# Three weight tiles side by side where a layer begins behind a norm

## The chip, the cores and the metric

One Trainium2 chip, one of its cores. The metric is the device time of one execution in microseconds (us); the median of three executions of the kernel before is 1987.98 us (1987.56 to 1994.38).

## The reference, cut to what matters

Two transformer-like blocks on 512 positions of 1024 features, all in float32. The first block is a pooling layer and a latent-attention layer; the second has an attention and an RWKV mixer that start from one normed input, and a convolutional feed-forward layer (ffn) behind a second norm. The change touches the two places of the second block where a norm is followed by large projections:

```python
h = rms_norm(x, norm1_w[l]) * (1.0 + sc1) + sh1
proj = h @ w_in[l]                      # mixers: 3 low-rank tiles of it are computed first
...
h = rms_norm(x, norm2_w[l]) * (1.0 + sc2) + sh2
x = x + gt2 * conv_ffn(h, w_up[l], conv_w[l], conv_b[l], w_down[l])   # starts with h @ w_up
```

## The kernel before, in words

Activations are held transposed: a tile has 128 features on the partitions and the 512 positions as columns, so 1024 features are eight tiles. To reach float32 accuracy every operand is split into a high part (rounded to TensorE's fp32r) and a low part (the rest), and each product is three matmuls: high weight x high activation (L176), high x low (L177), low x high (L178). One output tile over eight input tiles is 24 matmuls of 512 columns.

Weights come as chunks of 128x1024 (512 KB). `wload` (L137 and on) has SP transfer a chunk into one of three buffers "wraw", lets ScalarE copy it to "whi" (L160) and VectorE subtract to "wlo" (L161), both at high priority; whi and wlo have two buffers each. So up to three chunks are under way or waiting and two are split. The instructions' order on every engine and queue is set by a planner: it plays the program through and takes, of what is ready on an engine, what stands first in the program; what is written under `high_priority()` goes ahead of the rest. A tile's buffer is given when its first instruction is taken, and on the chip each engine and queue then runs its list in order. Pages of 128x512 come from pools that are opened and closed by stage: `pg1` (46 pages) up to the end of `Block2In.finish`, `pg4` (61 pages) from `attn_out` on. Between them lie the mixer's pools.

A norm works in halves of 256 columns: sums of squares (`Sums.add`, L318 and L320), column sums on TensorE (`norm_sum`, L262), root and reciprocal (`norm_end`), and the result spread over all partitions by a matmul with a diagonal (`spread`, L290 and L293) into a PSUM bank "ch". `modulate` then makes each of the eight tiles' high and low part: VectorE L738, ScalarE L739, VectorE L743. In the first norm three tiles of each half have the low part done by GpSimd (L742) behind an extra ScalarE pass (L741).

`gemm_head` is what follows. It loads the chunks of two output tiles with the subtraction on GpSimd instead of VectorE, and multiplies them half by half, one output tile after the other, into the two PSUM banks "mm". Further tiles follow over the full width, in the banks "sc": one (w_rw 26) in the mixers' head, two (w_up 2 and 3) in the ffn's, of which the first has its split in four pages "xwh" and "xwl", with the subtractions on GpSimd (L228). The results are taken from PSUM by `feat` (L816, L817) in the mixers and by `conv` (L1482 to L1484) in the ffn.

Ahead of the first head, `mla_layer` does the last output projections (`project`, chunks of w_mout), the last two of them in halves (`gemm_tail`). Ahead of the second, `attn_out` multiplies eight tiles by w_o, the last two in halves; its x comes by eight transfers "xf" into pages.

Of the kernel before, what the change touches and what calls it, by code (L numbers as in the profile page):

```python
# [9 lines left out]
AF = mybir.ActivationFunctionType  # L10
ALU = mybir.AluOpType
# [38 lines left out]
def f(ap):  # L50
    return ap.bitcast(F32)


class Kern:
# [155 lines left out]
                self.gemm_w(w, acts, ps[:, 0:S // 2], ts)  # L210
                evac(n, ps[:, 0:S // 2], ts)

    def gemm_head(self, wname, chunks, kts, acts, more=(), page=None):

        ws = []
        for c in chunks:
            ws.append(self.wchunks(wname, c, kts, self.nc.gpsimd))

        extra = None
        if page is not None:  # L220
            nc = self.nc
            raw = self.wp.tile([P, D], F32, name="wraw", tag="wraw")
            nc.sync.dma_start(raw, self.a[wname][more[0]][:, :D])
            extra = []
            for h in range(2):
                hi, lo, r = page(F32R, "xwh"), page(F32R, "xwl"), raw[:, h * S:h * S + S]
                nc.scalar.activation(hi, r, AF.Copy)
                nc.gpsimd.tensor_tensor(lo, r, f(hi), ALU.subtract)  # L228
                extra.append((hi, lo, 4))
        out = [self.mm() for _ in chunks]  # L230
        for ts in HALVES:
            for w, ps in zip(ws, out):
                self.gemm_w(w, acts, ps[:, ts], ts)
        for c in more:
            ps = self.bank("sc")
            self.gemm_w(extra or self.wchunks(wname, c, kts), acts, ps)
            extra = None
            out.append(ps)
        return out

    def gemm_multi(self, wname, chunk, kt, nt, acts, evac, n0):
# [234 lines left out]
def mla_layer(K, xs, mi, z_scr, done, after, filler=lambda h: None):  # L476
# [193 lines left out]
    def project(q, c, ys):  # L670

        K.gemm_multi("w_mout", 4 * q + c, 4, 2, ys[4 * q:4 * q + 4], evac_last if q == 3 else evac_x, 2 * c)
# [10 lines left out]
    for g in range(8):  # L683
        rope_split(*qrs[g])
        if g % 2 and g < 7:
            qrs += rope_q(g // 2 + 1)
        heads(g, o, ys)
        if g < 7:
            o = gemms(g + 1)
        if g == 7:  # L690
            flush()
            while vals:
                vals.pop(0)(None)
        for q, c in PROJ[g]:
            project(q, c, ys)
    for c in range(2):
        project(3, c, ys)
    ws = []
# [31 lines left out]
    nc.vector.scalar_tensor_tensor(K.A2, K.ada[:, 32:40], 1.0, K.v("norm2_w", 0, 8), ALU.add, ALU.mult)  # L730


def modulate(K, x, A, inv, sh, hl, ts=FULL, pool=False):

    nc = K.nc
    t = K.page(name="mod")[:, ts]
    hi, lo = hl[0][:, ts], hl[1][:, ts]
    nc.vector.scalar_tensor_tensor(t, x[:, ts], A, inv, ALU.mult, ALU.mult)  # L738
    ins = nc.scalar.activation(hi, t, AF.Identity, bias=sh)  # L739
    if pool:  # L740
        nc.scalar.activation(t, t, AF.Identity, bias=sh)  # L741
        return ins, nc.gpsimd.tensor_tensor(lo, t, f(hi), ALU.subtract)  # L742
    return ins, nc.vector.scalar_tensor_tensor(lo, t, sh, f(hi), ALU.add, ALU.subtract)  # L743


class Block2In:
# [10 lines left out]
    def finish(self):  # L757

        K, xs = self.K, self.xs
        nc = K.nc  # L760
        fa = K.const.tile([P, 8], F32, name="fa1")
        nc.vector.tensor_tensor(fa, K.A1, K.v("final_norm", 0, 8), ALU.mult)
        hs = [(K.apage("hh"), K.apage("hl")) for i in range(DT)]
        r1s = K.const.tile([P, 4], F32, name="r1s")
        hh = []
        for h, ts in enumerate(HALVES):

            nps = K.norm_sum([self.s1.last(), self.s2.last()], ts)
            ss = K.sm.tile([P, 2], F32, name="ss", tag="ss")
            with K.tc.high_priority():  # L770
                ins = nc.vector.tensor_scalar(ss, nps[:, 0:2], EPS, EPS * EPS * D, ALU.mult, ALU.add)
                for a in hh[2:3]:
                    K.behind(ins, a[1])
                nc.vector.tensor_tensor(ss, ss, nps[:, 2:4], ALU.add)
            r12 = K.norm_end(ss, D, 2, 0.0, [a[0] for a in hh[1:2]])
            inv12 = K.spread(r12, 2)
            nc.vector.tensor_copy(r1s[:, 2 * h:2 * h + 2], nps[:, 0:2])
            for i in range(DT):
                hh.append(modulate(K, xs[i], fa[:, i:i + 1], inv12, K.ada[:, i:i + 1], hs[i], ts, i in ((2, 4, 6), (1, 3, 5))[h]))
        r1s = K.norm_end(r1s, D)  # L780
        inv1 = K.spread(r1s)
        for i in range(DT):
            xf = K.page(name="xf")
            nc.vector.scalar_tensor_tensor(xf, xs[i], K.v("final_norm", i), inv1, ALU.mult, ALU.mult)
            nc.sync.dma_start(K.x_scr[i], xf)
        return hs


def rwkv(K, hs, filler=lambda: None):
# [19 lines left out]
    def feat(n, ps=None):  # L809

        if ps is None:
            ps = K.mm()
            K.gemm_n("w_rw", n, [8], hs, ps)
        z = K.page(name="zm")
        with K.tc.high_priority():
            nc.scalar.activation(z, ps, AF.Copy, scale=omu[:, n:n + 1])  # L816
            nc.vector.scalar_tensor_tensor(z[:, 1:], ps[:, :S - 1], K.v("mu", n), z[:, 1:], ALU.mult, ALU.add)  # L817
        return z

    pss = K.gemm_head("w_rw", (24, 25), [8], hs, (26,))  # L820
    zs_ = [feat(24 + i, ps) for i, ps in enumerate(pss)]

    lw = zs_[0]
    nc.scalar.activation(lw[0:64], lw[0:64], AF.Tanh)
# [617 lines left out]
def attn_out(K, mg, xscr):  # L1442

    nc = K.nc
    xs, xf = [], []
    acc = Sums(K)
    for n in range(DT):
        t = K.page(name="xf")
        nc.sync.dma_start(t, xscr[n])
        xf.append(t)  # L1450
        xs.append(K.page(name="x"))

    def evac(n, ps, ts=FULL):
        nc.vector.scalar_tensor_tensor(xs[n][:, ts], ps, K.ada[:, 16 + n:17 + n], xf[n][:, ts], ALU.mult, ALU.add)
        acc.add(n, xs[n], ts=ts)

    for n in range(DT - 2):
        ps = K.mm()
        K.gemm_n("w_o", n, [8], mg, ps)
        evac(n, ps)  # L1460
    K.gemm_tail([(n, K.wchunks("w_o", n, [8])) for n in (DT - 2, DT - 1)], mg, evac, acc.last())
    return xs, acc


def ffn(K, xs, acc):

    nc = K.nc
    hs = [(K.apage("hh"), K.apage("hl")) for i in range(DT)]
    for ts in HALVES:
        inv = K.rstd(acc.last(), D, ts)  # L1470
        for i in range(DT):
            modulate(K, xs[i], K.A2[:, i:i + 1], inv, K.ada[:, 24 + i:25 + i], hs[i], ts)

    def conv(n, ps=None):

        ci = (n % 2) * 22 + n // 2
        if ps is None:
            ps = K.mm()
            K.gemm_n("w_up", n, [8], hs, ps)
        t = K.page(name="cv")  # L1480
        w = [K.v("conv_w", j * 44 + ci) for j in range(3)]
        nc.scalar.activation(t, ps, AF.Identity, scale=w[2], bias=K.v("conv_b", ci))  # L1482
        nc.vector.scalar_tensor_tensor(t[:, 1:], ps[:, :S - 1], w[1], t[:, 1:], ALU.mult, ALU.add)
        nc.vector.scalar_tensor_tensor(t[:, 2:], ps[:, :S - 2], w[0], t[:, 2:], ALU.mult, ALU.add)  # L1484
        return t

    pss = K.gemm_head("w_up", (0, 1), [8], hs, (2, 3), K.page)
    for half in range(2):
        act = []
        for i in range(11):  # L1490
            n = 2 * (half * 11 + i)
            gt = conv(n, pss[n] if n < 4 else None)
            vl = conv(n + 1, pss[n + 1] if n < 4 else None)
            sg = K.page(name="sg")
            nc.scalar.activation(sg, gt, AF.Silu)
            a = K.page(name="fa")
            nc.vector.tensor_tensor(a, sg, vl, ALU.mult)
            act.append(K.split(a, "fa"))
        if half == 0:
            out = []  # L1500
            for n in range(DT):
                ps = K.mm()
                K.gemm_n("w_down", 2 * n, [6, 5], act, ps)
                x = K.page(name="x")
                nc.vector.scalar_tensor_tensor(x, ps, K.ada[:, 40 + n:41 + n], xs[n], ALU.mult, ALU.add)
                out.append(x)
            xs = out
    acc = Sums(K)
    xw = [K.page(name="xw") for n in range(DT)]

    def evac(n, ps, ts=FULL):
        x = xs[n][:, ts]
        nc.vector.scalar_tensor_tensor(x, ps, K.ada[:, 40 + n:41 + n], x, ALU.mult, ALU.add)  # L1513
        acc.add(n, xs[n], ts=ts)
        nc.gpsimd.tensor_scalar(xw[n][:, ts], x, K.v("norm_f_w", n), None, ALU.mult)

    for n in range(DT - 1):
        ps = K.mm()
        K.gemm_n("w_down", (DT + n) * 2, [6, 5], act, ps)
        evac(n, ps)  # L1520
    K.gemm_tail([(DT - 1, K.wchunks("w_down", (2 * DT - 1) * 2, [6, 5]))], act, evac, acc.last())
    return xw, acc
# [296 lines left out]
```

## Time and profile before

| | |
|---|---|
| median of three executions | 1987.98 us |
| the profiled execution | 1989.22 us |
| its span | 1987.4 us |
| TensorE matmul busy | 1915.4 us (96%) |
| VectorE busy | 1272.3 us (64%) |
| ScalarE busy | 890.4 us (45%) |
| GpSimd busy | 111.0 us (6%) |

The times that are argued with come from the profiled execution: positions are microseconds from the start of its span. In the profile PE is TensorE, PEld its weight loads, DVE is VectorE, ACT is ScalarE, POOL is GpSimd, and SP (SPq) is the queue that issues transfers. A timeline line has the start, the duration, the engine, the line of the code, the operation, output and inputs, sizes and count, and in brackets the engine's idle time before it and what ended it. Matmuls are pipelined, so their duration is longer than the distance of their starts.

### The profile page before, as it was taken

The page shows a single profiled execution, that of the slowest core. Times are in us where ns is not written, and L with a number is a line of the kernel's source. Part 1 is how long each engine was busy: PE and PEld are TensorE (multiplying, and loading weights), DVE is VectorE, ACT ScalarE, POOL GpSimd, SP SyncE. Part 2 cuts the span into 40 slices and gives each one's busy share as a digit, 9 for nine tenths or more (in the row PEclk, how much of TensorE's full clock was granted, in tenths as well). Part 3 has the DMA queues.
Part 4 walks back from the last instruction along what each step waited for, and adds up shares of the span by engine and source line. Part 5 has one row for each costly group of instructions (what it writes and reads, how often), then busy time and mean ns, then how long its engine had stood idle before and what let it go on. Part 6 is the DMA issues. An engine that isn't in the chain of part 4 may idle for free. (4 is left out here: it accounts for less than half of the span.)

```text
span 1987.4 us, 28348 instructions
## 1 busy us (share of the span) xinstructions
PE 1915.4 (96%) x10759; PEld 1553.2 (78%) x10771; DVE 1272.3 (64%) x2284; ACT 890.4 (45%) x1602; POOL 111.0 (6%) x221
## 2 busy tenths in 40 slices
PE   8999999999999998999999999989999999999998
PEld 6888887887888887777777866767777888888886
DVE  6746777768866668676567477466456576535654
ACT  5322333336655546543445555555642344423432
POOL 0000000000000002110030030020000010000002
PEclk9999999999999999999999999999999999999999
DMA  4332365675422223643443433334355423233322
GB/s 166 98 103 96 95 200 182 208 238 176 130 85 75 77 68 128 200 133 97 152 137 113 145 120 123 133 112 144 130 191 182 152 75 97 89 101 106 96 84 86
DMA packets 97496, 254.55 MB, mean 128 GB/s; under 512 B 11216, under 2 KB 15824, under 8 KB 97360
## 3 DMA queue, kind: packets, MB, share of 16 engines
q1 hardware_dynamic: 96848, 251.51, 39.6%
q8 instruction: 85, 1.39, 0.3%
q0 software_dynamic: 224, 0.79, 0.1%
q10 hardware_dynamic: 288, 0.45, 0.1%
q14 instruction: 51, 0.42, 0.1%
HBM read 212.59 MB, written 37.75 MB: 126 GB/s over the span
## 5 line engine op out<-in xcount | busy, mean ns | idle before, releaser
L160 ACT ACTIVATE whi<-wraw 128x1024 fp32r<-128x1024 f32 (+4 forms) x302 | 299.1, 991 | 592.2 <-PE mm L177 373.8
L161 DVE TENSOR_TENSOR wlo<-wraw,whi 128x1024 fp32r<-128x1024 f32 (+4 forms) x298 | 338.3, 1136 | 196.3 <-ACT whi L160 192.6
L177 PE MATMUL mm<-hl,whi 128*128 128x512 f32 (+1 forms) x992 | 393.5, 397 | 4.0 <-DVE hl L743 3.7
L176 PE MATMUL mm<-hh,whi 128*128 128x512 f32 (+1 forms) x992 | 389.8, 394 | 0.0
L178 PE MATMUL mm<-hh,wlo 128*128 128x512 f32 (+1 forms) x992 | 388.0, 392 | 0.0
L177 PEld LDWEIGHTS mm<-hl,whi 128*128 128x128 f32 x992 | 189.2, 191 | 42.8 <-DVE hl L743 4.3
L176 PEld LDWEIGHTS mm<-hh,whi 128*128 128x128 f32 x992 | 189.1, 191 | 38.1 <-issue 2.0
L178 PEld LDWEIGHTS mm<-hh,wlo 128*128 128x128 f32 x992 | 189.5, 191 | 35.7 <-issue 2.2
L176 PE MATMUL mm<-xgh,whi 128*128 128x512 f32 x432 | 170.2, 394 | 7.5 <-ACT xgh L342 7.1
L177 PE MATMUL mm<-xgl,whi 128*128 128x512 f32 x432 | 171.0, 397 | 0.7 <-DVE xgl L343 0.7
L178 PE MATMUL mm<-xgh,wlo 128*128 128x512 f32 x432 | 169.4, 392 | 0.0
L176 PEld LDWEIGHTS mm<-xgh,whi 128*128 128x128 f32 x432 | 81.9, 190 | 25.6 <-ACT xgh L342 7.1
L176 PE MATMUL mm<-yh,whi 128*128 128x512 f32 (+1 forms) x256 | 98.3, 384 | 0.0
L177 PE MATMUL mm<-yl,whi 128*128 128x512 f32 (+1 forms) x256 | 98.1, 383 | 0.0
L178 PE MATMUL mm<-yh,wlo 128*128 128x512 f32 (+1 forms) x256 | 98.0, 383 | 0.0
L177 PEld LDWEIGHTS mm<-xgl,whi 128*128 128x128 f32 x432 | 81.9, 190 | 19.2 <-DVE xgl L343 1.6
L178 PEld LDWEIGHTS mm<-xgh,wlo 128*128 128x128 f32 x432 | 81.7, 189 | 18.0 <-issue 1.0
L720 DVE SCALAR_TENSOR_TENSOR adaw<-adaw,cb 128x1024 f32<-128x1024 f32 x48 | 58.7, 1223 | 33.6 <-DMA adaw<-in_w_ada 32.4
L177 PE MATMUL mm<-fal,whi 128*128 128x512 f32 (+1 forms) x176 | 67.3, 383 | 0.0
L178 PE MATMUL mm<-fah,wlo 128*128 128x512 f32 (+1 forms) x176 | 67.3, 383 | 0.0
L176 PE MATMUL mm<-fah,whi 128*128 128x512 f32 (+1 forms) x176 | 67.3, 382 | 0.0
L658 ACT ACTIVATE p<-sc,nm 128x128 f32<-128x128 f32 (+1 forms) x64 | 33.7, 527 | 58.2 <-DVE nm L655 46.1
(422 smaller groups left out, 3541.2 us busy)
## 6 DMA issues: line engine op xcount, KB each, us to landing
adaw<-in_w_ada SPq DMA_DIRECT2D x48, 512.0 KB, 4.1
wraw<-in_w_up SPq DMA_DIRECT2D x44, 512.0 KB, 3.6
wraw<-in_w_at SPq DMA_DIRECT2D x36, 512.0 KB, 3.7
wraw<-in_w_pin SPq DMA_DIRECT2D x32, 512.0 KB, 3.6
wraw<-in_w_rw SPq DMA_DIRECT2D x27, 512.0 KB, 4.0
wraw<-in_w_min SPq DMA_DIRECT2D x22, 512.0 KB, 4.4
a_scr<-aqkv SPq DMA_DIRECT2D x36, 256.0 KB, 2.2
aq<-a_scr SPq DMA_DIRECT2D x36, 256.0 KB, 3.7
```

The source lines that it names most:

```text
L160: nc.scalar.activation(hi, raw, AF.Copy)
L161: eng.tensor_tensor(lo, raw, f(hi), ALU.subtract)
L176: nc.tensor.matmul(out, wh, ah, start=first, stop=False)
L177: nc.tensor.matmul(out, wh, al, start=False, stop=False)
L178: nc.tensor.matmul(out, wl, ah, start=False, stop=last)
L658: nc.scalar.activation(p[:, :nk], sc[:, :nk], AF.Exp, bias=nm, scale=scale, accum_out=sm)
L720: nc.vector.scalar_tensor_tensor(w, w, 1.0, K.cb, ALU.mult, ALU.mult, accum_out=K.ada[:, i:i + 1])
```

## The change

`head_weights` is new. It transfers three chunks and splits each into two high and two low pages, on ScalarE and VectorE, at high priority; it is called well ahead of its use: in `mla_layer` before the last output projections (w_rw 24, 25, 26), and in `attn_out` after the second of the eight w_o tiles (w_up 0, 1, 2). `gemm_head` takes these, and computes three output tiles side by side in halves: for every input tile all three output tiles' matmuls, into the two "mm" banks and one "sc" bank. In the mixers it is called inside `Block2In.finish`, directly behind the modulation. The ffn's fourth tile (w_up 3) goes the ordinary way. `modulate` loses its GpSimd form.

```diff
-    def gemm_head(self, wname, chunks, kts, acts, more=(), page=None):
+    def head_weights(self, wname, chunks, page):
+
+        nc = self.nc
         ws = []
         for c in chunks:
-            ws.append(self.wchunks(wname, c, kts, self.nc.gpsimd))
...
             raw = self.wp.tile([P, D], F32, name="wraw", tag="wraw")
-            nc.sync.dma_start(raw, self.a[wname][more[0]][:, :D])
-            extra = []
+            nc.sync.dma_start(raw, self.a[wname][c][:, :D])
+            w = []
             for h in range(2):
                 hi, lo, r = page(F32R, "xwh"), page(F32R, "xwl"), raw[:, h * S:h * S + S]
-                nc.scalar.activation(hi, r, AF.Copy)
-                nc.gpsimd.tensor_tensor(lo, r, f(hi), ALU.subtract)
-                extra.append((hi, lo, 4))
-        out = [self.mm() for _ in chunks]
+                with self.tc.high_priority():
+                    nc.scalar.activation(hi, r, AF.Copy)
+                    nc.vector.tensor_tensor(lo, r, f(hi), ALU.subtract)
+                w.append((hi, lo, 4))
+            ws.append(w)
+        return ws
+
+    def gemm_head(self, ws, acts):
+
+        out = [self.mm(), self.mm(), self.bank("sc")][:len(ws)]
         for ts in HALVES:
-            for w, ps in zip(ws, out):
-                self.gemm_w(w, acts, ps[:, ts], ts)
-        for c in more:
-            ps = self.bank("sc")
-            self.gemm_w(extra or self.wchunks(wname, c, kts), acts, ps)
-            extra = None
-            out.append(ps)
+            for ci in range(2):
+                for j in range(4):
+                    sl = slice(j * P, (j + 1) * P)
+                    k = ci * 4 + j
+                    for w, ps in zip(ws, out):
+                        hi, lo, _ = w[ci]
+                        self.mm3(ps[:, ts], hi[:, sl], lo[:, sl], acts[k][0][:, ts], acts[k][1][:, ts], k == 0, k == 7)
         return out
...
         for q, c in PROJ[g]:
             project(q, c, ys)
+    K.head = K.head_weights("w_rw", (24, 25, 26), K.page)
     for c in range(2):
         project(3, c, ys)
...
-    if pool:
-        nc.scalar.activation(t, t, AF.Identity, bias=sh)
-        return ins, nc.gpsimd.tensor_tensor(lo, t, f(hi), ALU.subtract)
...
+        K.heads = K.gemm_head(K.head, hs)
         r1s = K.norm_end(r1s, D)
...
-    pss = K.gemm_head("w_rw", (24, 25), [8], hs, (26,))
-    zs_ = [feat(24 + i, ps) for i, ps in enumerate(pss)]
+    zs_ = [feat(24 + i, ps) for i, ps in enumerate(K.heads)]
...
         evac(n, ps)
+        if n == 1:
+            K.head = K.head_weights("w_up", (0, 1, 2), K.page)
...
-    pss = K.gemm_head("w_up", (0, 1), [8], hs, (2, 3), K.page)
+    pss = K.gemm_head(K.head, hs)
...
-            gt = conv(n, pss[n] if n < 4 else None)
-            vl = conv(n + 1, pss[n + 1] if n < 4 else None)
+            gt = conv(n, pss[n] if n < 3 else None)
+            vl = conv(n + 1, pss[n + 1] if n < 2 else None)
```

## Rows read from the trace of the kernel before

**Rows 1.** The page, busy time of each engine, its share and its instructions.
```profile
PE 1915.4 (96%) x10759; PEld 1553.2 (78%) x10771; DVE 1272.3 (64%) x2284; ACT 890.4 (45%) x1602; POOL 111.0 (6%) x221
```
**Rows 2.** Windows: length, busy time by engine (instructions), granted clock, DMA share, GB/s.
```profile
755.40:761.70 6.30, 1.58 (x7) 1.10 (x7) 6.30 (x16) 3.08 (x6) 2.46 (x1) 0.82 0.42 120
761.70:784.60 22.90, 21.86 (x130) 19.49 (x130) 20.43 (x43) 14.68 (x30) 4.64 (x6) 0.90 0.27 93
1606.50:1631.47 24.97, 21.29 (x128) 19.59 (x127) 20.74 (x40) 12.27 (x22) 6.02 (x4) 0.86 0.27 78
1610.00:1615.00 5.00, 4.44 (x20) 4.37 (x21) 4.01 (x11) 2.35 (x6) 0.23 (x1) 0.50 0.36 111
```
**Rows 3.** Timeline of TensorE, attn_out and the ffn's head.
```profile
1571.82 0.39 PE L176 MATMUL mm<-mh,whi 128*128 128x512 f32 x1
...
1610.56 0.58 PE L177 MATMUL mm<-hl,whi 128*128 128x256 f32 x1 [1.87 <-DVE hl L743]
...
1616.92 0.60 PE L293 MATMUL ch<-dg,ones 128*128 128x256 f32 x2
...
1621.06 0.28 PE L177 MATMUL mm<-hl,whi 128*128 128x256 f32 x1
1621.18 0.28 PE L178 MATMUL mm<-hh,wlo 128*128 128x256 f32 x1
...
1631.47 0.39 PE L176 MATMUL sc<-hh,whi 128*128 128x512 f32 x1
1631.70 0.39 PE L177 MATMUL sc<-hl,whi 128*128 128x512 f32 x1
```
**Rows 4.** Timeline of VectorE, the ffn's head.
```profile
1605.15 2.47 DVE L320 TENSOR_TENSOR sq<-sq 128x256 f32<-128x256 f32 x1
...
1608.33 2.18 DVE L743 SCALAR_TENSOR_TENSOR hl<-mod,ada,hh 128x256 fp32r<-128x256 f32 x1
...
1620.72 0.47 DVE L738 SCALAR_TENSOR_TENSOR mod<-x,A,ch 128x256 f32<-128x256 f32 x1
1621.11 0.47 DVE L743 SCALAR_TENSOR_TENSOR hl<-mod,ada,hh 128x256 fp32r<-128x256 f32 x1
```
**Rows 5.** Timeline of GpSimd, the ffn's head.
```profile
1607.76 2.46 POOL L161 TENSOR_TENSOR wlo<-wraw,whi 128x1024 fp32r<-128x1024 f32 x1 [0.42 <-ACT whi L160]
```
**Rows 6.** Timeline of VectorE, the mixers' head.
```profile
757.88 2.16 DVE L320 TENSOR_TENSOR sq<-sq 128x256 f32<-128x256 f32 x1
```
**Rows 7.** Half a chunk: tile xwh's copies (ns, min/median/max), VectorE's timeline for a subtraction.
```profile
L227 ACT ACTIVATE xwh<-wraw x2: 617/618/618, 1623.2 to 1624.1; 128x512 fp32r<-128x512 f32 x2
...
1634.86 0.69 DVE L171 TENSOR_TENSOR fal<-fa,fah 128x512 fp32r<-128x512 f32 x1 [0.70 <-ACT fah L170]
```
**Rows 8.** Timeline of ScalarE, a result taken from PSUM in the ffn.
```profile
1643.29 0.76 ACT L1482 ACTIVATE cv<-mm,vec 128x512 f32<-128x512 f32 x1
```
**Rows 9.** Timeline of VectorE, a result taken from PSUM in the ffn.
```profile
1644.56 0.74 DVE L1483 SCALAR_TENSOR_TENSOR cv<-mm,vec,cv 128x511 f32<-128x511 f32 x1
```
**Rows 10.** The page, DMA issues: count, KB each, median us from issue to landing.
```profile
wraw<-in_w_up SPq DMA_DIRECT2D x44, 512.0 KB, 3.6
```
**Rows 11.** Windows, as in rows 2, the last attention heads.
```profile
705.00:710.00 5.00, 4.78 (x42) 4.33 (x41) 3.91 (x14) 3.14 (x10) 0.00 (x0) 1.00 0.17 52
```
**Rows 12.** Timeline, first instructions on tiles of the mixer's new pools.
```profile
790.13 0.33 SPq L90 DMA_DIRECT2D gmask<-in_gmask  x1
790.15 0.31 ACT L96 ACTIVATE bonr<-cst 128x128 fp32r<-128x128 f32 x1 [3.95 <-DMA wraw<-in_w_g]
```
**Rows 13.** Timeline of SP, the end of the mixers and attn_out.
```profile
1548.72 14.78 SPq L148 DMA_DIRECT2D wraw<-in_w_o  x5
...
1565.82 3.65 SPq L1449 DMA_DIRECT2D xf<-x_scr  x8
1569.57 10.39 SPq L148 DMA_DIRECT2D wraw<-in_w_o  x3
```
**Rows 14.** Tile wraw, the one transfer issued from 1569.3 to 1574 us (us, min/median/max).
```profile
DMA to landing us min/median/max: 6.4/6.4/6.4
```

More of the change, by code (lines that the diff above doesn't have):

```diff
@@ L211, in gemm_tail @@
                 evac(n, ps[:, 0:S // 2], ts)
-    def gemm_head(self, wname, chunks, kts, acts, more=(), page=None):
+    def head_weights(self, wname, chunks, page):
+        nc = self.nc
         ws = []
         for c in chunks:
-            ws.append(self.wchunks(wname, c, kts, self.nc.gpsimd))
-        extra = None
-        if page is not None:
-            nc = self.nc
             raw = self.wp.tile([P, D], F32, name="wraw", tag="wraw")
-            nc.sync.dma_start(raw, self.a[wname][more[0]][:, :D])
-            extra = []
+            nc.sync.dma_start(raw, self.a[wname][c][:, :D])
+            w = []
             for h in range(2):
                 hi, lo, r = page(F32R, "xwh"), page(F32R, "xwl"), raw[:, h * S:h * S + S]
-                nc.scalar.activation(hi, r, AF.Copy)
-                nc.gpsimd.tensor_tensor(lo, r, f(hi), ALU.subtract)
-                extra.append((hi, lo, 4))
-        out = [self.mm() for _ in chunks]
-        for ts in HALVES:
-            for w, ps in zip(ws, out):
-                self.gemm_w(w, acts, ps[:, ts], ts)
-        for c in more:
-            ps = self.bank("sc")
-            self.gemm_w(extra or self.wchunks(wname, c, kts), acts, ps)
-            extra = None
-            out.append(ps)
+                with self.tc.high_priority():
[6 more added lines that the diff above has]
+        out = [self.mm(), self.mm(), self.bank("sc")][:len(ws)]
+        for ts in HALVES:
+            for ci in range(2):
[5 more added lines that the diff above has]
+                        self.mm3(ps[:, ts], hi[:, sl], lo[:, sl], acts[k][0][:, ts], acts[k][1][:, ts], k == 0, k == 7)
         return out
@@ L730, in ada_finish, with modulate @@
     nc.vector.scalar_tensor_tensor(K.A2, K.ada[:, 32:40], 1.0, K.v("norm2_w", 0, 8), ALU.add, ALU.mult)
-def modulate(K, x, A, inv, sh, hl, ts=FULL, pool=False):
+def modulate(K, x, A, inv, sh, hl, ts=FULL):
     nc = K.nc
@@ L778, in finish @@
             for i in range(DT):
-                hh.append(modulate(K, xs[i], fa[:, i:i + 1], inv12, K.ada[:, i:i + 1], hs[i], ts, i in ((2, 4, 6), (1, 3, 5))[h]))
+                hh.append(modulate(K, xs[i], fa[:, i:i + 1], inv12, K.ada[:, i:i + 1], hs[i], ts))
+        K.heads = K.gemm_head(K.head, hs)
         r1s = K.norm_end(r1s, D)
```

## The prediction

> **What bounds the kernel now.** The page's busy times come first [rows 1]: TensorE is busy for 1915.4 us of a span of 1987.4 us and every other engine for far less, so a change can only win where TensorE is idle or slow. The windows show two such places, both behind a norm [rows 2]. In the first, from 755.40 to 784.60 us (the head of block two, 29.2 us), TensorE is busy for 1.58 of the first 6.30 us, and then runs 22.90 us at a mean clock of 0.90. In the second, from 1606.50 to 1631.47 us (the head of the ffn, 24.97 us), it is busy for 21.29 us at 0.86; a window inside it has 0.50, the 1.2 GHz level, right after waits on "DVE hl" such as that of 1.87 us [rows 2, 3].
>
> What those stretches need is read from matmul starts [rows 3]: half-width matmuls follow each other at 0.12 us, full-width ones at 0.23 us. VectorE makes one modulated tile in two instructions, 0.39 us apart, so about 0.8 us a tile [rows 4]; a weight tile alone takes three matmuls of it, 0.36 us. One tile at a time, TensorE outruns VectorE twofold, and waits.
>
> VectorE is itself held up. The addition at 1605.15 takes 2.47 us and the low part at 1608.33 takes 2.18 us, where the undisturbed one takes 0.47 us [rows 4]; the second begins while GpSimd does its 2.46 us subtraction of a weight tile [rows 5]. That is 1.7 to 2.0 us each. The first head has the same pattern twice, one of them the 2.16 us addition [rows 6].
>
> **The change part by part.**
>
> *Three tiles side by side.* 3 tiles x 2 halves x 24 matmuls = 144 at 0.12 us = 17.3 us. Per modulated tile TensorE now has nine matmuls, 1.07 us, above VectorE's 0.8 us, so after the first tile it should no longer outrun it. The third tile in halves costs 48 x 0.12 = 5.8 us against 24 x 0.23 = 5.4 us, which is inside the 17.3 us. To these come the norm of the second half: its spread takes 0.6 us [rows 3], and I count its four column sums as the same, an estimate: 1.2 us.
>
> *No GpSimd in the heads.* Its locks go, but the work does not vanish. As the head's own weights no longer sit in the two whi/wlo buffers, those are free for the next two tiles, whose splits are at high priority and take the same places, now with the subtraction on VectorE: about 1.3 us each (twice 0.69 us of [rows 7]). Two locks of 1.7 to 2.0 us less two subtractions of 1.3 us leaves VectorE about 1 us better in a head, not 3.5 us. The modulation's three GpSimd tiles per half go to VectorE as 0.4 us each, and as many ScalarE passes go; paced by 1.07 us this is covered.
>
> *First head.* I let the first matmul come 2.0 us earlier (a lock or more goes, part of a subtraction comes), so 4.3 us instead of 6.30 us. Then 17.3 + 1.2, about 1.0 us for the third, full-width spread that lies in the stretch before too, and 2.3 us for the low clock, which I keep because 4 us without work still precede it (22.90 x 0.10): 26.1 us.
>
> *What is late next: banks.* The old order had full-width tiles in the "sc" banks behind the halves, during which the "mm" banks were emptied. Now all three end within 0.72 us and the next tile wants the first tile's bank. Emptying is one ScalarE pass and one VectorE pass in the first head, one and two in the ffn: 0.76 + 0.74, or 0.76 + 0.74 + 0.74 [rows 8, 9]; with 0.3 us of handing over and less 0.72 us, TensorE waits 1.1 and 1.8 us. So the first head takes 27.2 us: gain 2.0 us (bounds: 6 us if the low clock and all of the late start go; 0 if VectorE keeps the pace it had).
>
> *Ffn head.* 17.3 + 1.2 + 1.5 us of waits for the first two or three tiles = 20.0 us against 24.97 us, less 1.8 us for the bank: gain 3.2 us (bounds: a gain of 5.5 us; a loss of 1).
>
> *Early splits, first head.* Six ScalarE copies of 0.62 us and six VectorE subtractions of 0.69 us [rows 7] instead of two whole copies, two GpSimd subtractions and a late third. Their transfers now stand on SP's queue ahead of the last four w_mout chunks and take weight buffers that these had; a 512 KB transfer lands in 3.6 us [rows 10], the pages of that pool are long open, and the chunks are wanted some 20 us later, so I put nothing there. But the splits then fall into the last attention heads, where VectorE is busy for 3.91 and TensorE for 4.78 of 5 us [rows 11]. Cost between 0 (it goes into VectorE's idle 1.1 us) and 6 x 0.69 = 4.1 us (all on the chain); I take 0.5 us, since an output projection is there to fill TensorE's waits.
>
> *Early splits, ffn head.* Here I expect the price. The split pages belong to the pool that opens when the mixer's pools close. At the other such boundary, tiles of that new pool on different queues and engines all start at 790.13 to 790.15 us, together [rows 12]: a pool opens as a whole. The ffn's pool opens at 1565.82 us, when the eight "xf" transfers start [rows 13]. The weight buffers ("wraw") are three. Before, five w_o chunks went out from 1548.72 on, as the buffers came free, chunks 2 to 4 among them [rows 13]. In the new program order w_up 0 to 2 precede w_o 2: they take those three places, and cannot be split and freed before 1565.82. Chunk w_o 2 then stands on SP's queue behind the eight xf, where w_o 5 stood: 1569.57 us [rows 13]. That one landed after 6.4 us [rows 14], so at 1576.0. Its copy takes 1.2 us (twice 0.62), so TensorE has its first matmul at 1577.2, where it had it at 1571.82 [rows 3]: 5.4 us; the low part comes 1.3 us later, with only 0.45 us of matmuls to do: 0.8 us more. Behind such a gap the clock was at 0.50 over a whole 5 us window [rows 2]; I count 4.4 us of it, 2.2 us lost. Sum 8.4 us; bounds 0 (pages open earlier, or the chunk is let past) and 10.
>
> The Trainium skill (DMA: Bandwidth & Descriptors, section "Queues, rings and completion order") says that each DMA engine takes the descriptors of one issuing engine's ring in order. By that, w_o 2 waits behind all 2 MB of xf, as the 6.4 us of [rows 14] agree; did it not hold, 3.6 us [rows 10] would do and the sum would be 5.6 us instead of 8.4.
>
> **Sum.** The profiled execution took 1989.22 us (span 1987.4), 1.24 above the median of 1987.98. -2.0 - 3.2 + 0.5 + 8.4 = +3.7 us: 1992.9 by the profiled one, 1991.7 by the median. A measurement tells apart what is over 0.5%, 9.9 us, so this is no change.
>
> **Rivals.**
> 1. *w_o 2 does not wait.* For it: the boundary in [rows 12] lies over one old pool, that of the ffn over several, and pages over an emptied one may open sooner. Against it: the xf transfers waited to 1565.82 though the new pool is large. Without the 8.4 us: 1983.3; with the heads at their best (6 + 5.5 instead of 5.2), 1977.
> 2. *Slower: the heads win nothing and w_o 2 waits.* The place is VectorE's queue at each head's start: if the next tiles' two subtractions, 2.6 us, go ahead of the first low parts, these come as late as behind GpSimd's locks, TensorE starts in pieces and stays at the low clock. From the point where the ffn's first low part is no sooner than 1608.0 the head gives 0. Then the bank waits, 1.1 + 1.8, come on top: 2.9 + 8.4 + 0.5 = 11.8 us, 1999.8; with all of the attention's 4.1 us, 2003. For it: those splits did go first in both heads before. Against it: nine matmuls per tile leave VectorE 0.27 us a tile to catch up.
> 3. *The change does not do what it says:* pages or buffers come so late that the splits run at the head itself. Then about the old order, with the bank waits: +3 us, 1991.
>
> **How the numbers follow.** Forecast 0.50, rival 1 0.28, rival 2 0.14, rival 3 0.08. The range takes in most of rivals 1 and 2: 1979 to 2000. Faster by over 0.5% (under 1978) needs rival 1 with both heads near their best: 0.09. Slower by over 0.5% (over 1997.9) is rival 2: 0.14. Within: 0.77.
>
> **What would show it.** Right: a TensorE wait of 4 to 7 us before w_o's third tile, ended by ScalarE's whi copy, with three w_up transfers ahead of it on SP's queue; the ffn head about 20 us and the first about 26 us from the norm on; waits of 1 to 2 us behind each head on the bank's evacuation; no VectorE addition over 1 us in the heads. Wrong: w_o's tiles without a gap (rival 1), or "DVE hl" waits of over 1 us in the heads (rival 2).

## The result, and the profile after

The changed kernel takes 2000.6 us (median of eight executions), the kernel before 1987.0 us in the same session: a ratio of 1.0052, with an interval of 1.0034 to 1.0070 (the two medians alone would give 1.0068, inside it). It is slower by about 10 us. Forecast were +3.7 us and "no change"; the sign is right, the size is not. The median lies just above the range given (1979 to 2000); the ratio, put on the 1987.98 us that the forecast set out from, gives 1998.3 us, just inside it. The profiled execution took 1993.68 us (span 1991.9), 4.5 us over that of before; the medians differ by more.

The page of the changed kernel shows the same busy times as before [rows 1], but for GpSimd:

```profile
PE 1915.5 (96%) x10819; PEld 1552.4 (78%) x10819; DVE 1271.2 (64%) x2301; ACT 889.9 (45%) x1601; POOL 94.7 (5%) x209
```

So the time is again in where TensorE waits. Its waits in the mixers' head (engine, tile and line, what ended the wait; us in total, times, longest; line numbers are the changed kernel's own, so its ScalarE square is L320 and its high part L742):

```profile
PE mm L176 <- ACT hh L742: 3.5, 1, 3.5
PE mm L176 <- DVE zm L818: 1.0, 1, 1.0
```

From w_o to the ffn the kernel before has only waits on low parts, in the ffn's head:

```profile
PE mm L177 <- DVE hl L743: 3.7, 3, 1.9
```

and the changed kernel:

```profile
PE mm L176 <- ACT whi L160: 8.1, 1, 8.1
PE mm L176 <- DVE cv L1486: 2.4, 1, 2.4
PE mm L177 <- DVE hl L743: 0.3, 1, 0.3
```

The 1.0 and 2.4 us are the bank waits of the forecast (1.1 and 1.8). The third line is all that is left of waiting inside the ffn's head. The 8.1 us stand before w_o's third tile (TensorE's line, where the kernel before goes on at 1571.82 without a wait, [rows 3]):

```profile
1574.53 0.80 PE L176 MATMUL mm<-mh,whi 128*128 128x512 f32 x1 [8.10 <-ACT whi L160]
```

and there they were forecast, as 5.4 + 0.8. Windows of the changed kernel (columns as in [rows 2]):

```profile
754.50:759.63 5.13, 0.88 (x4) 0.30 (x2) 5.04 (x15) 3.02 (x7) 0.00 (x0) 0.81 0.59 188
759.63:782.50 22.87, 21.90 (x157) 21.16 (x157) 19.93 (x49) 9.36 (x20) 0.00 (x0) 0.89 0.15 54
1570.00:1575.00 5.00, 0.47 (x1) 0.47 (x2) 2.71 (x5) 2.06 (x3) 0.00 (x0) 0.51 0.74 244
1575.00:1580.00 5.00, 4.96 (x12) 3.41 (x12) 1.96 (x2) 1.06 (x1) 0.00 (x0) 0.50 0.56 184
1612.28:1634.30 22.02, 19.20 (x152) 18.27 (x151) 16.47 (x39) 9.94 (x20) 0.00 (x0) 1.00 0.16 48
1635.00:1640.00 5.00, 5.00 (x16) 3.91 (x16) 2.86 (x4) 2.45 (x4) 0.00 (x0) 0.67 0.00 2
```

Both heads are shorter: 28.0 us from the end of the work before to the next ordinary tile (754.50 to 782.50), where it was 29.2, and 22.02 us for 24.97 [rows 2]. In the ffn's head the clock is 1.00 where it was 0.86. Against that stand two places: a window at 0.67 behind the bank wait, and the wait in w_o with the half clock behind it. Over all of w_o the kernel before has 1.00:

```profile
1560.00:1605.00 45.00, 44.92 (x239) 38.55 (x238) 23.62 (x34) 15.60 (x22) 0.06 (x1) 1.00 0.41 141
```

Where w_o's chunk was, SP's timeline tells (before: [rows 13]):

```profile
1548.59 0.33 SPq L148 DMA_DIRECT2D wraw<-in_w_o  x1
1551.31 6.62 SPq L219 DMA_DIRECT2D wraw<-in_w_up  x3
1560.25 3.65 SPq L1449 DMA_DIRECT2D xf<-x_scr  x8
1569.84 15.85 SPq L148 DMA_DIRECT2D wraw<-in_w_o  x6
```

and ScalarE's:

```profile
1563.90 0.63 ACT L320 ACTIVATE sq<-x 128x512 f32<-128x512 f32 x1 [4.46 <-DVE x L1454]
1567.26 0.63 ACT L320 ACTIVATE sq<-x 128x512 f32<-128x512 f32 x1 [2.72 <-DVE x L1454]
1567.79 3.21 ACT L224 ACTIVATE xwh<-wraw 128x512 fp32r<-128x512 f32 x6
1573.42 1.06 ACT L160 ACTIVATE whi<-wraw 128x1024 fp32r<-128x1024 f32 x1 [2.42 <-DMA wraw<-in_w_o]
```

The pool opens at 1560.25, when the eight xf go out. The three w_up chunks sit in the three weight buffers and could be split from then on; but their copies start at 1567.79, 7.5 us later, directly behind the second tile's square. Only when the first is split does w_o's third chunk go out, at 1569.84, and TensorE, done with w_o's second tile, goes on at 1574.53.

### The profile page after: what moved, and what is told of

It reads as the page before. It is cut to its first block, busy times and chain, and to the rows that moved or that the text cites. A ratio compares the mean times of both kernels' runs of the same rounds, so it can differ in the third digit from the quotient of the medians.

```text
span 1991.9 us, 28446 instructions
## 1 busy us (share of the span) xinstructions
PE 1915.5 (96%) x10819; PEld 1552.4 (78%) x10819; DVE 1271.2 (64%) x2301; ACT 889.9 (45%) x1601; POOL 94.7 (5%) x209
## 5 line engine op out<-in xcount | busy, mean ns | idle before, releaser
L160 ACT ACTIVATE whi<-wraw 128x1024 fp32r<-128x1024 f32 (+3 forms) x297 | 294.0, 990 | 584.6 <-PE mm L177 369.8
L161 DVE TENSOR_TENSOR wlo<-wraw,whi 128x1024 fp32r<-128x1024 f32 (+3 forms) x297 | 337.1, 1135 | 199.1 <-ACT whi L160 194.5
L176 PE MATMUL mm<-hh,whi 128*128 128x512 f32 x936 | 373.7, 399 | 3.4 <-DVE cv L1486 2.4
L177 PE MATMUL mm<-hl,whi 128*128 128x512 f32 x936 | 375.4, 401 | 0.0
L178 PE MATMUL mm<-hh,wlo 128*128 128x512 f32 x936 | 371.8, 397 | 0.0
L176 PEld LDWEIGHTS mm<-hh,whi 128*128 128x128 f32 x936 | 176.8, 189 | 42.2 <-issue 4.3
L177 PEld LDWEIGHTS mm<-hl,whi 128*128 128x128 f32 x936 | 176.8, 189 | 37.9 <-issue 1.5
L178 PEld LDWEIGHTS mm<-hh,wlo 128*128 128x128 f32 x936 | 176.9, 189 | 36.1 <-issue 2.2
```

Of the source, the lines that this page charges most:

```text
L160: nc.scalar.activation(hi, raw, AF.Copy)
L161: eng.tensor_tensor(lo, raw, f(hi), ALU.subtract)
L176: nc.tensor.matmul(out, wh, ah, start=first, stop=False)
L177: nc.tensor.matmul(out, wh, al, start=False, stop=False)
L178: nc.tensor.matmul(out, wl, ah, start=False, stop=last)
```

## The experiments

Each ratio is to the kernel before, run on the same chip beside it, with a 95% interval. Besides the times, each profile was cut at four instructions that every version has, and the pieces compared: at the last "mh", at the ffn's first "hh" and at the first and the last "sg". They are read from three tiles' instructions on ScalarE (count, ns min/median/max, first and last start). The kernel before:

```profile
L1423 ACT ACTIVATE mh<-mt x8: 616/632/633, 1516.7 to 1564.4; 128x512 fp32r<-128x512 f32 x8
...
L739 ACT ACTIVATE hh<-mod,ada x16: 492/508/511, 1605.0 to 1623.7; 128x256 fp32r<-128x256 f32 x16
...
L1495 ACT ACTIVATE sg<-cv x22: 618/619/632, 1632.8 to 1915.7; 128x512 f32<-128x512 f32 x22
```

The changed kernel:

```profile
L1423 ACT ACTIVATE mh<-mt x8: 612/632/634, 1511.1 to 1558.8; 128x512 fp32r<-128x512 f32 x8
...
L742 ACT ACTIVATE hh<-mod,ada x16: 493/509/511, 1610.8 to 1626.0; 128x256 fp32r<-128x256 f32 x16
...
L1497 ACT ACTIVATE sg<-cv x22: 618/619/630, 1635.5 to 1920.2; 128x512 f32<-128x512 f32 x22
```

From the last "mh" to the first "hh" of the ffn is w_o with the norm: 1605.0 - 1564.4 = 40.6 us before, 52.0 after. From there to the first "sg" is the ffn's head: 27.8 and 24.7. From the first to the last "sg" is the rest of w_up's tiles, with the first half of w_down's among them: 282.9 and 284.7. For the mixers the piece goes from the first "pt" of the attention to the last "zm" of the projections, so that it holds the early splits as well as the head: 502.9 and 497.7. The columns below are these four, and the part from the last "mh" to the end:

| | ratio | mixers | w_o | ffn head | w_up | mh to end |
|---|---|---|---|---|---|---|
| before | 1 | 502.9 | 40.6 | 27.8 | 282.9 | 423.0 |
| the change | 1.0052 (1.0034 to 1.0070) | 497.7 | 52.0 | 24.7 | 284.7 | 433.1 |
| e1 the change again | 1.0052 (1.0034 to 1.0069) | 500.4 | 51.5 | 24.7 | 284.6 | 431.9 |
| e2 mixers' head alone | 1.0001 (0.9988 to 1.0014) | 497.6 | 40.6 | 28.1 | 282.9 | 423.2 |
| e3 ffn's head alone | 1.0045 (1.0026 to 1.0064) | 501.9 | 51.0 | 24.7 | 283.1 | 430.5 |
| e4 call after the fifth tile | 1.0035 (1.0023 to 1.0048) | 500.6 | 52.3 | 24.7 | 284.6 | 432.7 |
| e5 call ahead of the square | one run | 500.1 | 48.4 | 24.7 | 283.1 | 427.9 |
| e6 one chunk at a time | 0.9983 (0.9973 to 0.9993) | 500.8 | 41.1 | 24.7 | 283.1 | 420.1 |
| e7 one mm, two sc banks | 1.0011 (0.9996 to 1.0026) | 498.1 | 51.6 | 24.8 | 280.5 | 428.5 |
| e8 e6 and e7 together | 0.9958 (0.9944 to 0.9971) | 497.3 | 41.4 | 24.7 | 280.6 | 417.8 |
| e9 e8's ffn part alone | 0.9971 (0.9957 to 0.9986) | 501.2 | 41.0 | 24.7 | 280.6 | 417.4 |
| e10 mixers' head, banks | 0.9979 (0.9961 to 0.9996) | 498.7 | 40.7 | 28.0 | 282.9 | 423.2 |
| e11 e8 again | 0.9954 (0.9937 to 0.9970) | 497.8 | 41.7 | 24.8 | 280.5 | 418.6 |

The mixers' piece holds more than the head. It can be cut once more at the first "ip", a ScalarE pass some 30 us behind the head, here of the kernel before and then of the changed kernel:

```profile
L894 ACT ACTIVATE ip<-cs x3: 614/617/630, 815.5 to 990.1; 128x512 f32<-128x512 f32 x3
...
L894 ACT ACTIVATE ip<-cs x3: 615/617/629, 813.0 to 983.7; 128x512 f32<-128x512 f32 x3
```

From the first "pt" (475.3 and 474.1 us) to there it is 340.2 us before and 338.9 after. The three versions with the old head (before, e3, e9) have 340.2 to 341.5, 340.9 in the mean; the six with the new one (the change, e1, e2, e4, e5, e6) 338.8 to 340.2, 339.6 in the mean; the four with one mm and two sc banks (e7, e8, e10, e11) 337.9 to 339.1, 338.5 in the mean. So the mixers' part is worth 1.3 us, and 2.4 with the other banks, where versions with the same head differ by as much as 1.4. Behind the first "ip" all run the same part of the program, and yet the rest of the piece takes from 158.7 to 162.7 us: 162.7 before, 158.8 in the changed kernel. What differs there is the granted clock, as here (before, then the changed kernel around the same place):

```profile
915.00:925.00 10.00, 9.05 (x114) 7.00 (x114) 4.49 (x4) 6.39 (x12) 0.53 (x1) 0.66 0.47 138
...
900.00:940.00 40.00, 37.92 (x355) 29.41 (x354) 21.76 (x39) 18.23 (x35) 1.64 (x3) 1.00 0.37 110
```

The changed kernel has 158.8 us there and e6, with the same mixers, 161.2, so this is no part of the change. It is also why the two profiled executions lie only 4.5 us apart: the changed kernel loses 10.1 us from the last "mh" on and wins 1.3 up to "ip", but also 3.9 us behind "ip", and 0.4 elsewhere.

**e1, the changed kernel again.** No edit.

> The changed kernel once more, unaltered, for a second profile and more times. Theory A (the w_o chunk that was pushed behind three w_up chunks is what costs): TensorE's wait before w_o's third tile is there again, 7 to 9 us, and the time is 1992 to 2004 us. Rival B (that wait varies and makes the spread of the times): in a slower profile the wait is longer, 10 us or more. Rival C (the spread comes from somewhere else, by the granted clock): the wait is the same 8 us and another stretch, outside both heads, has a clock below 1 that it did not have.

Ratio 1.0052 once more, and the wait in w_o is 8.3 us against 8.1, though the span was 8.7 us longer than in the first profile: it is no matter of chance, and Rival B falls. Of the 8.7 us, 5.4 lie ahead of the attention's first "pt" (479.5 against 474.1 us) and 4.5 between there and the last "mh"; from then on the second profile is 1.2 us shorter. From 1375 to 1380 us its granted clock is 0.50, where the first profile has 1.00 from 1350 to 1380: that is Rival C. So much do two executions of one kernel differ, away from what was changed.

**e2 and e3, each head alone.** In e2 the ffn, in e3 the mixers keep the head of the kernel before (under another name), its GpSimd tiles and its late loads with it.

```diff
-    pss = K.gemm_head(K.head, hs)
+    pss = K.gemm_head_old("w_up", (0, 1), [8], hs, (2, 3), K.page)
```

```diff
-    K.head = K.head_weights("w_rw", (24, 25, 26), K.page)
...
-        K.heads = K.gemm_head(K.head, hs)
...
-    zs_ = [feat(24 + i, ps) for i, ps in enumerate(K.heads)]
+    pss = K.gemm_head_old("w_rw", (24, 25), [8], hs, (26,))
+    zs_ = [feat(24 + i, ps) for i, ps in enumerate(pss)]
```

> Only the mixers' head changed, the ffn's head as before. Theory A: the mixers' head brings 1 to 3 us net of its bank wait, so 1984 to 1987 us, and no wait before w_o's third tile. Rival D (the early splits in the last attention heads cost more than the head brings): 1989 to 1995 us.

> Only the ffn's head changed, the mixers' head as before. Theory A: 8.1 us of wait, 3 us behind it (low part and low clock), less 3.4 us from the head: 7 to 8 us slower than before, 1994 to 1996 us. Rival D: most of the loss sits in the other head, so within 2 us of before.

e2 comes out even. Its interval reaches from a gain of 2.4 us to a loss of 2.8, so its times alone decide between neither theory; the 1.3 us won up to "ip" are for Theory A, and there is no wait in w_o. The loss is the ffn part's, with w_o's wait at 8.3 us in e3.

**e4, the call moved behind the fifth w_o tile**, where the pool is long open:

```diff
-        if n == 1:
+        if n == 4:
             K.head = K.head_weights("w_up", (0, 1, 2), K.page)
```

> The changed kernel with the w_up chunks asked for after the fifth w_o tile instead of the second, so that five w_o chunks stand ahead of them. Theory A: no wait of over 1 us before w_o's third tile, about 11 us less than the changed kernel: 1985 to 1990 us. Rival E (the ffn's head itself, its next tiles' splits and the bank wait, is what costs): within 3 us of the changed kernel, 1996 to 2001 us.

This expectation failed: the wait is 8.4 us, now before w_o's sixth tile. SP's timeline:

```profile
1550.71 14.78 SPq L148 DMA_DIRECT2D wraw<-in_w_o  x5
1567.82 3.65 SPq L1449 DMA_DIRECT2D xf<-x_scr  x8
1571.56 10.39 SPq L219 DMA_DIRECT2D wraw<-in_w_up  x3
1593.71 2.73 SPq L148 DMA_DIRECT2D wraw<-in_w_o  x3
```

ScalarE's:

```profile
1591.12 0.63 ACT L320 ACTIVATE sq<-x 128x512 f32<-128x512 f32 x1 [4.81 <-DVE x L1454]
1591.66 3.21 ACT L224 ACTIVATE xwh<-wraw 128x512 fp32r<-128x512 f32 x6
1597.59 1.06 ACT L160 ACTIVATE whi<-wraw 128x1024 fp32r<-128x1024 f32 x1 [2.72 <-DMA wraw<-in_w_o]
```

The pool had been open for 24 us, and no xf is near. Still the copies come directly behind the square of the tile after which they are called, and w_o's sixth chunk goes out 2.1 us behind their start. So neither the pool nor the xf is the cause. The new theory: the planner does not take the splits, at whatever priority, ahead of the square that precedes them in the program (both take pages of one pool), and until then three unsplit chunks hold all three weight buffers. The order and the buffers are tried below; that the shared pool is the planner's reason for the order is argued from the code, and no run shows it.

**e5, the call one place earlier**, ahead of the second tile's addition and square:

```diff
         K.gemm_n("w_o", n, [8], mg, ps)
-        evac(n, ps)
         if n == 1:
             K.head = K.head_weights("w_up", (0, 1, 2), K.page)
+        evac(n, ps)
```

> The call for w_up's three chunks stands ahead of the second w_o tile's addition and square instead of behind them; nothing else differs. Theory A (a page is handed out in program order, so the six splits cannot go ahead of the square that took its page before them): the copies now begin behind the first tile's square, at about 1564.5 us instead of 1567.8, the first weight buffer is free some 3.3 us sooner, and TensorE's wait before w_o's third tile falls from 8.1 to 4 to 5.5 us; the time falls by about 3 us. Theory B (the splits wait for the pool to open or for a transfer): they stay at about 1567.8 and the wait at 8 us. Theory C (w_o's third chunk is late because it stands behind the eight xf on SP's queue): the splits come sooner, the wait stays at 8 us.

ScalarE's timeline:

```profile
1572.28 0.63 ACT L320 ACTIVATE sq<-x 128x512 f32<-128x512 f32 x1 [4.53 <-DVE x L1454]
1572.81 3.22 ACT L224 ACTIVATE xwh<-wraw 128x512 fp32r<-128x512 f32 x6
1577.86 0.63 ACT L320 ACTIVATE sq<-x 128x512 f32<-128x512 f32 x1 [1.83 <-DVE x L1454]
1579.26 1.06 ACT L160 ACTIVATE whi<-wraw 128x1024 fp32r<-128x1024 f32 x1 [0.77 <-DMA wraw<-in_w_o]
```

The copies now come directly behind the first square, 4.3 us after the xf go out at 1568.56 instead of 7.5, and TensorE's wait is 5.6 us. That is just above the 4 to 5.5 us of Theory A; B and C said 8. From the last "mh" to the end e5 takes 427.9 us where the change takes 431.9 to 433.1.

**e6, one chunk at a time**, behind tiles 0, 2 and 4, so that never all three buffers hold chunks that can't be split:

```diff
-        if n == 1:
-            K.head = K.head_weights("w_up", (0, 1, 2), K.page)
+        if n in (0, 2, 4):
+            K.head += K.head_weights("w_up", (n // 2,), K.page)
```

> w_up's three chunks are asked for one by one, behind w_o's tiles 0, 2 and 4, instead of together behind tile 1. Theory A (three weight buffers held at once by chunks that cannot be split yet are what delays w_o's chunk): no w_o chunk is late, no wait of TensorE over 1 us in w_o's tiles; the 8.1 us go, and some 3 us of low clock and of waiting for low parts with them, so 11 us less than with the three together: within 0.3% of the kernel before (ratio 0.997 to 1.001), the bank wait of 2.4 us behind the ffn's head still there. Theory B (any w_up chunk among w_o's costs its wait until the pool is open): a wait of 3 to 8 us moves to a later tile of w_o, ratio 1.003 to 1.005. What the ffn's head takes (about 21.6 us with its bank wait) should not change by either.

All that TensorE waits for from w_o to the ffn:

```profile
PE mm L176 <- DVE cv L1486: 2.4, 1, 2.4
PE mm L177 <- DVE hl L743: 0.4, 1, 0.4
```

SP's timeline of e6 (the second and third w_up chunk, and the w_o chunks behind the xf):

```profile
1564.84 0.33 SPq L219 DMA_DIRECT2D wraw<-in_w_up  x1
1567.49 3.65 SPq L1449 DMA_DIRECT2D xf<-x_scr  x8
1571.23 2.74 SPq L148 DMA_DIRECT2D wraw<-in_w_o  x2
1579.63 0.33 SPq L219 DMA_DIRECT2D wraw<-in_w_up  x1
```

and ScalarE's, where the copies come in pairs behind the first and the third square:

```profile
1571.13 0.63 ACT L320 ACTIVATE sq<-x 128x512 f32<-128x512 f32 x1 [2.04 <-DVE x L1454]
1571.67 1.14 ACT L224 ACTIVATE xwh<-wraw 128x512 fp32r<-128x512 f32 x2
...
1577.29 1.06 ACT L160 ACTIVATE whi<-wraw 128x1024 fp32r<-128x1024 f32 x1 [2.17 <-DMA wraw<-in_w_o]
...
1580.30 0.63 ACT L320 ACTIVATE sq<-x 128x512 f32<-128x512 f32 x1 [0.28 <-DVE x L1454]
1580.84 1.14 ACT L224 ACTIVATE xwh<-wraw 128x512 fp32r<-128x512 f32 x2
```

w_o takes 41.1 us for 40.6 before, and the kernel is faster than before by 0.17%. The six splits, 3.2 us of ScalarE and 3.7 us of VectorE, are all still there: by themselves they cost TensorE 0.5 us (0.4 to 1.1 in e6, e8, e9 and e11). The wait and the half clock, 52.0 - 41.1 = 10.9 us, were those of the buffers.

**e7 and e8, the banks.** The three tiles take one "mm" and two "sc" banks:

```diff
-        out = [self.mm(), self.mm(), self.bank("sc")][:len(ws)]
+        out = [self.mm(), self.bank("sc"), self.bank("sc")][:len(ws)]
```

> The head's three tiles use one mm bank and two sc banks instead of two and one, so the next tile finds an mm bank free. Theory: the bank waits, 2.4 us behind the ffn's head and 1.0 us behind the mixers', go; w_o's wait of 8 us stays; the time is 3.4 us under the changed kernel's, ratio to the kernel before 1.003 to 1.004. Rival (the next tile's low part or the second half's emptying is late next): the wait turns into one of 1 to 2 us on a wlo or on an sc bank, and the ratio stays at 1.0045 to 1.006.

> Both edits: w_up's chunks one by one behind tiles 0, 2 and 4, and one mm and two sc banks in the heads. Theory: neither the 8.1 us wait nor the bank waits: 14.4 us under the changed kernel, so 3 to 5 us under the kernel before, ratio 0.9975 to 0.9985; the heads then show what they are worth by themselves. Rival (the heads gain nothing by themselves, what was won in them is lost to the splits that moved into the attention and w_o): ratio 0.9995 to 1.001.

Neither bank wait appears in e7 or e8, and w_o's wait is 8.3 us in e7 and none in e8. In w_up's piece this is worth 283.1 - 280.5 = 2.6 us, up to the mixers' first "ip" about 1 us (means of 339.6 and 338.5 us). By these pieces e7 is 5.5 - 2.4 = 3.1 us above before and e8 5.2 + 2.4 = 7.6 us below it; measured are 1.0011 (2.2 us) and 0.9958 (8.3 us), and both intervals hold what the pieces give. Both are better than either theory had them: the theories set out from the changed kernel's measured loss of 10 us, where the pieces of its two profiles have 7.6 to 8.8 us (10.1 and 8.9 from the last "mh" on, less 1.3), and counted the bank wait of the ffn without the low clock that stood behind it there, 1.5 us. e8 beats both kernels.

**e9, e10 and e11: e8's two halves, and e8 again.**

> The mixers' head is that of the kernel before; the ffn's head is the new one with w_up's chunks asked for one by one and with one mm and two sc banks. Theory: from the traces the stretch from w_o to the end is 5.2 us shorter (417.8 against 423.0 us), so a ratio of 0.9968 to 0.998. Rival (most of the 8 us that the mended kernel wins comes from the mixers' head): 0.999 to 1.000.

> The ffn's head is that of the kernel before; the mixers' head is the new one with one mm and two sc banks. Theory: without the bank wait of 1.0 us and its emptying, the new mixers' head gives 2 to 2.5 us and the early splits in the attention take about 1 us of it: ratio 0.9985 to 0.9998. Rival (a gain of 3 us or more there): 0.997 to 0.9984.

> The mended kernel once more, w_up's chunks one by one and one mm and two sc banks, beside its two halves. If the halves add up, its ratio is the product of theirs, 0.9955 to 0.9975; no wait of TensorE over 1 us in w_o and none on a bank behind the heads.

The ffn's half comes out as expected, 0.9971. That of the mixers, 0.9979, lies in the rival's range (3 us or more), with an interval that reaches into the theory's; the 2.4 us up to "ip" would be 0.9988, in the theory's. Between the two nothing here decides. The product of the halves is 0.9950 and e11 has 0.9954, a hair below the range that was expected: they add up. In e11 TensorE waits for no more than 0.5 us in w_o, and on no bank behind the heads.

## Why the prediction was right and wrong

**Right: the direction and its mechanism.** The heads win and w_o's third tile pays more than they win (e2 and e3 tell the two apart). The three w_up transfers stand ahead of the chunk on SP's queue, the wait is ended by ScalarE's whi copy, and it is found where it was put.

**Right: the ffn's head.** A gain of 3.2 us net of the bank wait was forecast; the pieces give 27.8 - 24.7 = 3.1 and, with w_up's at 283.1 (e3, e5, e6) for 282.9, 2.9 us. VectorE's long instructions beside GpSimd, 2.47 and 2.18 us [rows 4], are gone; no modulation in the new head takes over 0.48 us, and no addition of either norm over 0.69 us. The next tiles' two subtractions came at the head's start as argued (changed kernel, VectorE):

```profile
1610.62 1.23 DVE L161 TENSOR_TENSOR wlo<-wraw,whi 128x1024 fp32r<-128x1024 f32 x1
1612.10 0.48 DVE L743 SCALAR_TENSOR_TENSOR hl<-mod,ada,hh 128x256 fp32r<-128x256 f32 x1
...
1613.67 1.22 DVE L161 TENSOR_TENSOR wlo<-wraw,whi 128x1024 fp32r<-128x1024 f32 x1
```

Rival 2, by which these would eat the gain, falls by the 0.3 us of "hl" waits; rival 1 by the wait in w_o; rival 3 by the splits, which end some 40 us before the ffn's head starts.

**Near: the mixers' part.** -2.0 + 0.5 = -1.5 us was forecast. Up to the first "ip" it is -1.3; the times of e2 say +0.2, give or take 2.6. Inside, the head takes 28.0 us where 27.2 were forecast: its first matmul comes 5.13 us behind the work before, where 4.3 us were put (6.30 before), and the 22.87 us from there on are what the forecast's terms add up to (22.9). The 0.5 us for the early splits are too small to be told apart.

**Wrong: the size of "Early splits, ffn head", 8.4 us.** The step said that the chunks "cannot be split and freed before 1565.82", that is until the pool opens, and that w_o 2 then stands behind the eight xf. They were held longer, to the second square, 7.5 us behind the opening. So the chunk went out 9.6 us behind the first xf, where 3.75 us were taken from [rows 13], and with the xf gone it landed in 3.6 us, not 6.4 [rows 14]. 5.8 us later and 2.8 us quicker make 8.4 us of the 5.4; 8.1 were measured. The 0.8 us for the low part did not come; the half clock cost 2.7 us (from 1574.53 to 1580 at 0.50) where 2.2 was taken. Together 10.8 us, and 10.9 by e6 (52.0 - 41.1), above the step's own upper bound of 10. [Rows 12] and [rows 13] show when a pool opens; nothing was read for what stands between the opening and the split on ScalarE's list, and that the program's squares come first was there in the code.

The forecast weighed the Trainium skill (DMA: Bandwidth & Descriptors, section "Queues, rings and completion order") for the landing behind the xf. In the changed kernel the rule was not in play. In e6 it was: the fourth chunk is issued at 1571.23, right behind the xf of 1567.49, and its copy starts at 1577.29, 6.1 us later and released by that transfer. The traces agree with the rule; what was wrong was that w_o's chunk would go out right behind the xf.

**Wrong: the bank wait as a wait alone.** 2.4 us for 1.8 is close. But in the changed kernel, e1 and e4 the granted clock dropped behind it (0.67 in the window shown above), and w_up's piece is 1.5 us longer than in e3, e5 and e6, where the same 2.4 us leave it at 1.00. This was not in the sum.

**The sum.** By the pieces of its first profile: w_o +11.4, head -3.1, w_up +1.8, mixers -1.3, so +8.8 us in place of +3.7. The profile of e1 gives 8.9 - 1.3 = +7.6. The measured 10.3 us has an interval from 6.8 to 13.9 us, which holds both; what of it is above 8.8 us is not placed and may be noise. By its time the kernel stands where rival 2 was put (over 1997.9 us, chance 0.14), but not by rival 2's mechanism, since both heads win. The range reached so far because of that rival, so it was luck that the time of the forecast's own path came to its edge and not beyond.

## What to carry to other kernels

Work that is brought forward takes its buffers forward too: ask of each how long it is held by a load that cannot be used yet, and who is next in line for it. Three buffers given at once to loads that were split late cost 10.9 us here; given one at a time, the same work cost 0.4 to 1.1. When several results end together, look where the next one gets its bank: one changed name was worth 2.6 us in one head and about 1 in the other. Before a piece of one profile is put down to a change, look at the granted clock in it: here it moved the mixers' piece by more than the change did.

## What was not expected of the hardware

A gap of 2.4 us on TensorE, the same in six executions, was followed by a lower granted clock in three of them (means of 0.67, 0.68 and 0.84 over the 5 us window in which the fall begins, so a stay at 1.2 GHz inside it) and by none in the other three. Where it was, w_up's piece is 1.5 us longer. The four executions without the gap (e7, e8, e9, e11) have w_up's piece alike within 0.1 us. That it is the gap that lowers the clock is not shown: three executions with the same gap go on at 1.00, and the clock fell elsewhere too, as to 0.66 from 915 to 925 us in the kernel before and to 0.50 from 1375 to 1380 us in e1, where the changed kernel's first profile has 1.00. Behind the gap of 8.1 us the clock stood at 0.50, the 1.2 GHz level, for 5.5 us or so of dense matmuls in the changed kernel.
